# Stick-breaking attention layer: start of the kernel reordered, parked splits moved in the queues, some VectorE work moved to GpSimd

## The chip, the cores and the metric

The kernel runs on one core of a Trainium2 chip. The metric is device time in microseconds (us) of one launch. The engines of the core are TensorE (PE in the profile, PEld for its weight loads), VectorE (DVE), ScalarE (ACT) and GpSimd (POOL). SyncE (SP) only issues transfers (DMAs). Every engine works its own instructions in the order of the program and waits for the others by semaphores.

## What is computed

One layer of an encoder (DEPTH is 1, so only mixer 0 is used) on 2048 tokens of 1024 features, all float32:

```python
def stick_breaking_mixer(h, w_qkv, w_o):
    qkv = (h @ w_qkv).reshape(b, s, 3, N_HEADS, HEAD_DIM)
    q, k, v = qkv[:, :, 0], qkv[:, :, 1], qkv[:, :, 2]
    ...
        z = jnp.einsum('bthd,bshd->bhts', q[:, q0:end], k[:, :end]).astype(jnp.float32) * scale
        ...
        sp = jnp.where(mask, jax.nn.softplus(z), 0.0)
        rest = lax.cumsum(sp, axis=3, reverse=True)
        log_a = jnp.where(mask, z - rest, -jnp.inf)
        a = jnp.exp(log_a).astype(v.dtype)
        outs.append(jnp.einsum('bhts,bshd->bthd', a, v[:, :end]))
    ...
    return o @ w_o
...
    mod_all = jnp.einsum('bd,lde->lbe', jax.nn.silu(c), ada_w) + ada_b[:, None]
    ...
        sh_m, sc_m, gt_m, sh_f, sc_f, gt_f = jnp.split(mod_all[i][:, None, :], 6, axis=-1)
        h = modulate(rms_norm(x, norm_g[i, 0]), sh_m, sc_m)
        y = stick_breaking_mixer(h, sb_w_qkv[r], sb_w_o[r])
        x = x + gt_m * rms_norm(y, norm_g[i, 1])
        h = modulate(rms_norm(x, norm_g[i, 2]), sh_f, sc_f)
        y = swiglu_ffn(h, ffn_w_in[i], ffn_w_out[i])
        x = x + gt_f * rms_norm(y, norm_g[i, 3])
```

There are 16 heads of 64 features (8 pairs of heads), and the FFN is 2816 wide.

## The kernel before, in words

**Splits.** Products keep float32 accuracy by splitting each operand into a high part (a cast to fp32r, mostly on ACT) and a low part (operand minus high part, mostly on DVE); `mm3` then makes three matmuls for each product (its three are lines 254 to 256). Tokens stand in four blocks of 512 (b = 0 to 3), heads in eight pairs (p = 0 to 7).

**The start (from line 988).** The first transfers bring c, the biases and gains of the modulation, x of block 0, c as one row, and rows of the modulation's weights mixed with the first weights of q, k and v. PE runs `warm` matmuls, whose result nobody reads, spreads c over all partitions (`c_spread`, line 1016), and runs more of them. `x_square` (ACT, line 245), a power on GpSimd (249) and `x_scale` (DVE, 433) normalize x. `row_sum` (881) and `column` (873) make the shift and scale of one block of 128 features after another; `turn_x`, `full`, `high`, `low` make the modulated input h, and `products(p, m)` adds feature block m into the q, k and v of token block 0, for head pairs 0 and 1 at once (`EARLY`). `weights_high` and `weights_low` split the weights, in two halves of features each.

**The parked pair.** The q, k and v of (p=1, b=0) are made at the start but used much later. `project` splits them by functions put on the list `waiting` and stores them to DRAM (`k_park`, `q_park`, `v_s`); `unpark` brings them back. The v of head pair 1 stands in a tile with the tag `vn`, of which there is **one buffer** (`BUFS["vn"]` is 1): `take_values(b, half, acc)` copies the high parts on ACT (line 716) and makes the low parts on DVE (718) for pair 0 and pair 1, and after the second half it issues the store of pair 1's tile (722). The next block's `take_values` writes the same buffer, and so waits for that store.

**Order.** PE, ACT, DVE and GpSimd run what is written, in that order. `project(at)` yields one slice after each feature block; t = 1 is k, t = 0 is q, t = 2 and 3 are the halves of v. `at` = 2 is (p=0, b=1). Within it `X_AT` and `NORM_AT` hang the norm of blocks 2 and 3 on slices (squares, scales, loads, and `first_norm`, which turns and modulates one feature block). SP's transfers all go through one hardware queue; their order is the scheduler's.

**After attention.** `out_projection(b)` multiplies by w_o; beside it `o_load`, `o_add`, `o_prep` add and split the two partial attention outputs of the next block, `y_square`, `y_gate`, `y_norm`, `x1_add`, `x1_square`, `x1_scale`, `h2_turn` make the residual and the FFN's input. The FFN follows, with `end_square`, `end_mean`, `end_norm`, `end_store` at its end.

Of the kernel before, what the change touches and what calls it, by code (L numbers as in the profile page):

```python
# [11 lines left out]
AF = mybir.ActivationFunctionType  # L12
ALU = mybir.AluOpType
# [133 lines left out]

NORM_IN_KEYS = {1: {0: 4, 1: 5, 2: 6, 3: 7}, 2: {0: 5, 1: 6, 3: 7}, 3: {0: 5, 1: 6, 3: 7}}

H_FETCH_AT = [0, 2, 4, 6]  # L150
# [3 lines left out]
def f32(ap):  # L154
    return ap.bitcast(F32)
# [22 lines left out]
def hybrid_trunk_kernel(  # L178
# [20 lines left out]
    nc = tc.nc  # L199
# [11 lines left out]
    ones = const.tile([P, P], F32, name="ones")  # L211
# [59 lines left out]
    raws = {}  # L271
# [271 lines left out]
    def project(at):  # L543
# [17 lines left out]
        def product(t):  # L561
# [3 lines left out]
            for k in range(KC):  # L565
                if t == 1 and p == 0:
                    first_norm(b, NORM_IN_KEYS[b].get(k, KC))
                    if k >= 4 and waiting:
                        waiting.pop(0)()
                for what, *which in X_AT.get((at, t, k), []):  # L570
# [53 lines left out]
        def split(acc, tag):  # L624
            place = "wraw" if parked else "qkn"
            hl = att.tile([P, 2, BT], F32R, name=f"{tag}n{p}_{b}", tag=place, bufs=BUFS[place])
            nc.scalar.copy(hl[:, 0], acc)
            nc.vector.tensor_tensor(hl[:, 1], acc, f32(hl[:, 0]), op=ALU.subtract)
            return hl
# [4 lines left out]
        if parked:  # L634
            for out_of in held:
                nc.sync.dma_start(*out_of)
            for t, to in ((1, k_park), (0, q_park)):
                waiting.append(
                    lambda t=t, to=to: nc.sync.dma_start(to, f32(split(first_acc[p, t], "qk"[t])))
                )  # L640
            for half in range(2):
                waiting.append(lambda half=half: take_values(0, half, first_acc["v", half]))
            return
# [283 lines left out]
    def weights_low(half, *which):  # L927
        ks = K_HALVES[half]
        for of in which:
            if of == "v":  # L930
                hl = value_split[half]
                nc.vector.tensor_tensor(hl[:, 1], raws.pop(("v", 0, half)), f32(hl[:, 0]), op=ALU.subtract)
                continue
            p, t = of
            hi, lo = weights[p, t]
            raw = raws[p, t] if half == 0 else raws.pop((p, t))
            nc.vector.tensor_tensor(lo[:, ks], raw[:, ks], f32(hi[:, ks]), op=ALU.subtract)

# [49 lines left out]
    c_line = att.tile([P, D], F32, name="c_line", tag="qkn", bufs=BUFS["qkn"])  # L988
    nc.vector.memset(c_line, 0.0)
    nc.sync.dma_start(c_act, c)  # L990
    nc.sync.dma_start(b_cols, ada_b_cols)
    nc.sync.dma_start(gc, g_cols)
    x_load(0, 0)
    x_load(0, 1)
    nc.sync.dma_start(c_line[0:1], c_row)
    x_load(0, 2)
    x_load(0, 3)
    pairs = [[(0, 1), (0, 0)], [(1, 1), (1, 0), "v"]]
    row_load(0)
    weights_load(0, *pairs[0])  # L1000
    row_load(1)
    weights_load(0, *pairs[1])
# [12 lines left out]
    for half in range(2):  # L1015
        nc.tensor.matmul(c_spread[half], ones, c_line[:, c_halves[half]], start=True, stop=True)
    warm(11)
    x_square(0, 0)
    x_square(0, 1)
    x_scale(0, 0)  # L1020
    c_rows = att.tile([P, D], F32, name="c_rows", tag="qkn", bufs=BUFS["qkn"])
    for half in range(2):
        nc.scalar.activation(c_rows[:, c_halves[half]], c_spread[half], AF.Sigmoid)
    for half in range(2):
        nc.vector.tensor_tensor(
            c_rows[:, c_halves[half]], c_spread[half], c_rows[:, c_halves[half]], op=ALU.mult
        )
    x_scale(0, 1)
    x_square(0, 2)
    row_sum(0, 0)  # L1030
    x_square(0, 3)
    x_scale(0, 2)
    row_sum(0, 1)
    x_scale(0, 3)
    row_done(0)
# [3 lines left out]
    }  # L1039
    weights_high(0, *pairs[0])  # L1040
    turn_x(0)
    turn_x(1)
    full(0)
    weights_low(0, *pairs[0])
    high(0)
    low(0)
    acol = zps.tile([P, BT], F32, name="acol", tag="z")
    column(1, 0)
    products(0, 0)
    column(1, 1)  # L1050
# [62 lines left out]
    low(5)  # L1113
    x_load(2, 0, 1)
    store(2)
# [14 lines left out]
    high(7)  # L1130
    x_load(2, 2, 3)
    products(0, 5)
# [89 lines left out]
    def y_gate(i):  # L1222
        t = y_gated[0, i, 0]
        nc.vector.tensor_tensor(t, t, gate[0], op=ALU.mult)

# [46 lines left out]
    def o_add(b, k):  # L1272
        parts = o_parts.pop((b, k))
        o = att.tile([P, BT], F32, name=f"of{b}_{k}", tag="tmp", bufs=BUFS["tmp"])
        eng = nc.vector if b else nc.gpsimd
        eng.tensor_tensor(o, parts[:, 0], parts[:, 1], op=ALU.add)
        o_sum[b, k] = o
# [548 lines left out]
    def end_norm(s, i, j):  # L1826
        rstd = att.tile([P, 1], F32, name=f"e{s}_{i}_{j}_rstd", tag="rms_rstd", bufs=4)
        ms = att.tile([P, 1], F32, name=f"e{s}_{i}_{j}_sum", tag="rms_ms2", bufs=4)
        nc.vector.tensor_scalar(
            ms, end_ssq.pop((s, i, j)).pop(), end_ms.pop((s, i, j)), None, op0=ALU.add  # L1830
        )
        nc.gpsimd.tensor_tensor(rstd, ms, mhalf, op=ALU.pow)
        end_rstd[s, i, j] = rstd
# [140 lines left out]
```

## Time and profile before

| what | value |
|---|---|
| median of 3 runs | 2821.14 us (2820.8 to 2825.9) |
| the profiled execution's own time | 2822.93 us |
| its span | 2821.1 us |
| mean granted TensorE clock | 0.999 |
| DVE, ACT, POOL busy | 72%, 57%, 45% of the span |
| HBM | 360.48 MB read, 128.45 MB written, 173 GB/s over the span |

Each row of a profile's groups or timeline has the line of the kernel, the engine, the operation and what it writes and reads (out<-in, with buffer numbers left out), then busy time and idle time before it with the instruction or transfer that ended the idle time. Table rows by stretch give the busy microseconds of each engine, the granted clock, the share of the 16 DMA engines that was busy, and GB/s.

### The profile page before, as it was taken

The numbers are of one execution on the slowest core, as the hardware profiler recorded it, in microseconds if no ns is written. First come the engines' busy times: TensorE is split into PE (matmuls) and PEld (weight loads), VectorE is DVE, ScalarE is ACT, GpSimd is POOL, SyncE is SP. The second block draws the span as 40 slices with busy tenths as digits, with TensorE's granted clock in tenths as the row PEclk, the third lists the DMA queues.
The fourth block names the chain that finished last, engine by engine and source line by source line (L and its number), as shares of the span: only waits on it lengthen the run. The fifth ranks groups of instructions, "written<-read, shape, count | busy, mean of one in ns | idle before, by whom it ended". The sixth has DMA issues, their size and how long they took to land.

```text
span 2821.1 us, 42833 instructions
## 1 busy us (share of the span) xinstructions
PE 2787.4 (99%) x14297; PEld 2351.6 (83%) x14297; DVE 2024.4 (72%) x2841; ACT 1620.9 (57%) x3262; POOL 1276.2 (45%) x2031
## 2 busy tenths in 40 slices
PE   9999999999999999999999999999999999999998
PEld 7888888888888888888787888888888888888887
DVE  7788898888898888889767766555786665133467
ACT  5687777777787878788645533334433334322343
POOL 1475666666676656667310122222222222544454
PEclk9999999999999999999999999999999999999999
DMA  9866567786678745364489545335363335645565
GB/s 376 309 218 195 152 220 230 226 267 222 197 260 271 229 144 189 122 202 157 140 286 316 169 150 160 106 112 168 119 191 111 91 112 164 197 143 151 179 226 186
DMA packets 252096, 540.53 MB, mean 192 GB/s; under 512 B 23393, under 2 KB 117601, under 8 KB 234978
## 3 DMA queue, kind: packets, MB, share of 16 engines
q1 hardware_dynamic: 251874, 537.78, 59.2%
q8 instruction: 113, 1.85, 0.3%
q14 instruction: 109, 0.89, 0.1%
HBM read 360.48 MB, written 128.45 MB: 173 GB/s over the span
## 4 chain that ended last, share of the span: by engine, by line
PE 81%; DMA 6%; DVE 6%; issue 3%; POOL 2%; ACT 2%; SPq 1%; DVEq 0%; POOLq 0%; ACTq 0%
PE s L254 9%; PE s L256 9%; PE s L255 9%; PE o L837 8%; PE z L758 8%; PE t L809 8%; PE pj L254 5%; PE pj L256 5%; PE pj L255 5%; PE o L255 4%; PE o L256 4%; PE o L254 4%; DMA xc<-in_xt 1%; PE y L256 1%; PE y L254 1%
## 5 line engine op out<-in xcount | busy, mean ns | idle before, releaser
L799 POOL TENSOR_TENSOR a<-a,w 128x512 f32<-128x512 f32 (+3 forms) x640 | 620.0, 969 | 221.5 <-DVE w L792 121.4
L792 DVE TENSOR_TENSOR_SCAN w<-z,c,begin 128x512 f32<-128x512 f32 x384 | 488.7, 1278 | 76.0 <-ACT z L777 62.1
L254 PE MATMUL s<-r,l 128*128 128x512 f32 x1232 | 481.4, 391 | 1.6 <-ACT p L1647 1.4
L256 PE MATMUL s<-r,l 128*128 128x512 f32 x1232 | 479.6, 389 | 0.0
L255 PE MATMUL s<-r,l 128*128 128x512 f32 x1232 | 479.4, 389 | 0.0
L775 ACT ACTIVATE a<-z 128x512 f32<-128x512 f32 (+3 forms) x640 | 347.4, 543 | 165.0 <-PE z L758 141.5
L837 PE MATMUL o<-aT,v 128*128 128x512 f32 (+3 forms) x1280 | 384.6, 382 | 0.0
L825 DVE TENSOR_TENSOR aT<-t,aT 128x512 fp32r<-128x512 f32 (+3 forms) x640 | 358.9, 596 | 19.8 <-ACT aT L819 18.8
L758 PE MATMUL z<-kt,qt 128*128 128x512 f32 (+3 forms) x1280 | 363.1, 365 | 0.6 <-DVE n_ms L247 0.6
L819 ACT CAST aT<-t 128x512 fp32r<-128x512 f32 (+3 forms) x640 | 312.7, 533 | 77.7 <-PE t L809 62.1
L777 ACT ACTIVATE z<-z 128x512 f32<-128x512 f32 (+3 forms) x640 | 345.0, 539 | 0.0
L1711 POOL TENSOR_TENSOR one<-p,p 128x512 f32<-128x512 f32 x44 | 70.5, 1603 | 574.4 <-issue 303.7
L809 PE MATMUL t<-begin,a 128*128 128x128 f32 x2176 | 295.7, 273 | 9.9 <-DVE aT L825 8.4
L809 PEld LDWEIGHTS t<-begin,a 128*128 128x128 f32 x2176 | 252.8, 140 | 52.7 <-DVE aT L825 12.5
L254 PEld LDWEIGHTS s<-r,l 128*128 128x128 f32 x1232 | 231.3, 188 | 51.4 <-ACT p L1647 2.2
L256 PEld LDWEIGHTS s<-r,l 128*128 128x128 f32 x1232 | 231.3, 188 | 48.4 <-DVE l L1564 0.4
L255 PEld LDWEIGHTS s<-r,l 128*128 128x128 f32 x1232 | 231.3, 188 | 48.2 <-issue 0.5
L758 PEld LDWEIGHTS z<-kt,qt 128*128 128x128 f32 x1280 | 230.2, 188 | 38.3 <-DVE n_ms L247 1.0
L787 DVE TENSOR_TENSOR_SCAN w<-z,begin 128x128 f32<-128x128 f32 (+3 forms) x256 | 208.3, 817 | 73.5 <-ACT z L777 57.7
L1564 DVE TENSOR_TENSOR l<-ls,l 128x512 fp32r<-128x512 f32 x172 | 129.5, 753 | 155.0 <-ACT l L1563 154.7
L837 PEld LDWEIGHTS o<-aT,v 128*128 128x128 f32 x1280 | 214.2, 190 | 23.8 <-issue 0.7
L254 PE MATMUL pj<-ht,w 128*128 128x512 f32 x576 | 230.0, 399 | 0.2 <-DVE ht L481 0.2
(195 smaller groups left out, 5373.1 us busy)
## 6 DMA issues: line engine op xcount, KB each, us to landing
ht<-h_s SPq DMA_DIRECT2D x108, 1024.0 KB, 7.7
wi<-in_win SPq DMA_DIRECT2D x86, 512.0 KB, 4.3
qt<-qn SPq DMA_DIRECT2D x124, 256.0 KB, 4.4
ol_qt<-act_s SPq DMA_DIRECT2D x56, 512.0 KB, 3.8
act_s<-S SPq DMA_DIRECT2D x66, 256.0 KB, 5.0
br<-in_wout SPq DMA_DIRECT2D x66, 256.0 KB, 3.6
h_s<-ht SPq DMA_DIRECT2D x16, 1024.0 KB, 10.0
o_s<-os SPq DMA_DIRECT2D x128, 128.0 KB, 3.2
```

The source lines that it names most:

```text
L254: nc.tensor.matmul(acc, lhs[0], rhs[0], start=first, stop=False, **kw)
L255: nc.tensor.matmul(acc, lhs[0], rhs[1], start=False, stop=False, **kw)
L256: nc.tensor.matmul(acc, lhs[1], rhs[0], start=False, stop=last, **kw)
L758: nc.tensor.matmul(z[:, :n], q[:, e, part, r * P : (r + 1) * P], k[:, e, :n], start=part == 0, stop=part == 1,)
L775: nc.scalar.activation(a[:, :n], z[:, :n], AF.Sigmoid, scale=QK_SCALE)
L777: nc.scalar.activation(z[:, :n], z[:, :n], AF.Sigmoid, scale=-QK_SCALE)
L792: nc.vector.tensor_tensor_scan(rest[:, rev], left[:, rev], begin[:, :BT][:, rev], initial=carries[r], op0=ALU.mult, op1=ALU.bypass,)
L799: nc.gpsimd.tensor_tensor(a[:, :n], a[:, :n], rest[:, 1 : n + 1], op=ALU.mult)
L809: nc.tensor.transpose(pt[:, rb * P : (rb + 1) * P], weighed[i, rb][:, j * P : (j + 1) * P], ident)
L819: nc.scalar.copy(hl[:, 0, t0:], pt[:, t0:])
L825: nc.vector.tensor_tensor(hl[:, 1, t0:], pt[:, t0:], f32(hl[:, 0, t0:]), op=ALU.subtract)
L837: nc.tensor.matmul(acc[:, t0:], lhs, hl[:, part, t0:], start=sc == qb and j == 0 and part == 0, stop=sc == 0 and j == 3 and part == 1,)
```

## The change

The start: the order of the first transfers, of the squares, of the weight splits and of one `column` is changed, c is spread with one row of ones instead of 128, two of the `x_scale` go to ACT, two `warm` matmuls go, and the second halves of the weights' low parts are made on GpSimd. The parked splits: their slices are given by `WAITING_AT` (at, t, k), values first, and their tiles have the tag `aT` instead of `wraw`. After attention: `y_gate` and, for block 1, `o_add` go to GpSimd, and the sum in `end_norm` too.

```diff
+WAITING_AT = [(2, 0, 1), (2, 0, 4), (2, 2, 0), (2, 2, 3)]
...
                 if t == 1 and p == 0:
                     first_norm(b, NORM_IN_KEYS[b].get(k, KC))
-                    if k >= 4 and waiting:
-                        waiting.pop(0)()
+                if (at, t, k) in WAITING_AT:
+                    waiting[WAITING_AT.index((at, t, k))]()
...
         def split(acc, tag):
-            place = "wraw" if parked else "qkn"
+            place = "aT" if parked else "qkn"
...
-            for t, to in ((1, k_park), (0, q_park)):
-                waiting.append(
-                    lambda t=t, to=to: nc.sync.dma_start(to, f32(split(first_acc[p, t], "qk"[t])))
-                )
-            for half in range(2):
-                waiting.append(lambda half=half: take_values(0, half, first_acc["v", half]))
+            park = lambda t, to: nc.sync.dma_start(to, f32(split(first_acc[p, t], "qk"[t])))
+            waiting.extend([
+                lambda: take_values(0, 0, first_acc["v", 0]), lambda: park(1, k_park),
+                lambda: park(0, q_park), lambda: take_values(0, 1, first_acc["v", 1]),
+            ])
             return
...
-                nc.vector.tensor_tensor(hl[:, 1], raws.pop(("v", 0, half)), f32(hl[:, 0]), op=ALU.subtract)
+                eng = nc.gpsimd if half else nc.vector
+                eng.tensor_tensor(hl[:, 1], raws.pop(("v", 0, half)), f32(hl[:, 0]), op=ALU.subtract)
...
-            nc.vector.tensor_tensor(lo[:, ks], raw[:, ks], f32(hi[:, ks]), op=ALU.subtract)
+            eng = nc.gpsimd if half else nc.vector
+            eng.tensor_tensor(lo[:, ks], raw[:, ks], f32(hi[:, ks]), op=ALU.subtract)
...
-    nc.vector.memset(c_line, 0.0)
     nc.sync.dma_start(c_act, c)
-    nc.sync.dma_start(b_cols, ada_b_cols)
-    nc.sync.dma_start(gc, g_cols)
-    x_load(0, 0)
-    x_load(0, 1)
     nc.sync.dma_start(c_line[0:1], c_row)
-    x_load(0, 2)
-    x_load(0, 3)
+    for i in range(4):
+        x_load(0, i)
     pairs = [[(0, 1), (0, 0)], [(1, 1), (1, 0), "v"]]
     row_load(0)
     weights_load(0, *pairs[0])
+    nc.sync.dma_start(b_cols, ada_b_cols)
+    nc.sync.dma_start(gc, g_cols)
...
-        nc.tensor.matmul(c_spread[half], ones, c_line[:, c_halves[half]], start=True, stop=True)
-    warm(11)
-    x_square(0, 0)
-    x_square(0, 1)
-    x_scale(0, 0)
+        nc.tensor.matmul(c_spread[half], ones[0:1], c_line[0:1, c_halves[half]], start=True, stop=True)
+    warm(9)
...
+    for i in range(4):
+        x_square(0, i)
+    x_scale(0, 0)
     x_scale(0, 1)
-    x_square(0, 2)
+    for i in range(2, 4):
+        nc.scalar.activation(x_norm[0, i], x_tiles.pop((0, i)), AF.Identity, scale=x_rstd.pop((0, i)))
     row_sum(0, 0)
-    x_square(0, 3)
-    x_scale(0, 2)
     row_sum(0, 1)
-    x_scale(0, 3)
     row_done(0)
...
-    weights_high(0, *pairs[0])
+    weights_high(0, pairs[0][0])
     turn_x(0)
     turn_x(1)
     full(0)
-    weights_low(0, *pairs[0])
+    weights_low(0, pairs[0][0])
     high(0)
+    weights_high(0, pairs[0][1])
     low(0)
+    weights_low(0, pairs[0][1])
     acol = zps.tile([P, BT], F32, name="acol", tag="z")
+    products(0, 0)
     column(1, 0)
-    products(0, 0)
     column(1, 1)
...
-    x_load(2, 0, 1)
...
-    x_load(2, 2, 3)
+    x_load(2)
...
     def y_gate(i):
         t = y_gated[0, i, 0]
-        nc.vector.tensor_tensor(t, t, gate[0], op=ALU.mult)
+        nc.gpsimd.tensor_tensor(t, t, gate[0], op=ALU.mult)
...
-        eng = nc.vector if b else nc.gpsimd
+        eng = nc.vector if b > 1 else nc.gpsimd
...
-        nc.vector.tensor_scalar(
-            ms, end_ssq.pop((s, i, j)).pop(), end_ms.pop((s, i, j)), None, op0=ALU.add
-        )
+        nc.gpsimd.tensor_tensor(ms, end_ssq.pop((s, i, j)).pop(), end_ms.pop((s, i, j)), op=ALU.add)
         nc.gpsimd.tensor_tensor(rstd, ms, mhalf, op=ALU.pow)
```

Three places in the order of the instructions. In the rows, `kn_1`, `qn_1` and `v_1` are of token block 1, `kn_0`, `qn_0` and `v_0` (the two buffers of `take_values`, pair 0 and pair 1) are the parked ones of block 0; x_0 to x_3 are four token tiles.

SP's queue from the last stores of h of block 1 on, before (`h_s_107` is h of block 2, `x_0` to `x_2` here are x of block 3):

```order
L523 DMA h_s_106<-ht_1_3_773 128x2048
L639 DMA k_park<-kn_0_785 128x1024
L639 DMA q_park<-qn_0_799 128x1024
L722 DMA v_s_0_85<-v_0_813 128x1024
L653 DMA kt_1_846<-kn_1_843 64x512 x4
L410 DMA x_0_853<-in_x 128x1024
L410 DMA x_1_855<-in_x 128x1024
L410 DMA x_2_857<-in_x 128x1024 x2
L662 DMA qt_1_898<-qn_1_895 64x1024 x4
L523 DMA h_s_107<-ht_2_0_879 128x2048
```

The same stretch of SP's queue in the changed kernel:

```order
L525 DMA h_s_106<-ht_1_3_770 128x2048
L654 DMA kt_1_824<-kn_1_821 64x512 x4
L412 DMA x_0_831<-in_x 128x1024
L412 DMA x_1_833<-in_x 128x1024
L412 DMA x_2_835<-in_x 128x1024 x2
L639 DMA k_park<-kn_0_857 128x1024
L663 DMA qt_1_886<-qn_1_883 64x1024 x4
L639 DMA q_park<-qn_0_892 128x1024
L525 DMA h_s_107<-ht_2_0_867 128x2048
L723 DMA v_s_0_85<-v_0_842 128x1024
```

The store of the parked v (`v_s_0`) moved from the third transfer after h of block 1 to the last of these, behind keys, x of block 3, queries and one store of h of block 2.

ACT around the parked values in the changed kernel (lines 717 and 482 are 716 and 480 of before):

```order
L717 CAST v_0_841<-pj_0_2_370 128x4x64
L717 CAST v_0_842<-pj_0_2_370 128x4x64
L717 CAST v_1_959<-pj_1_2_891 128x4x64
L717 CAST v_1_960<-pj_1_2_891 128x4x64
L482 ACTIVATE hf_2_982<-xT_2_983,mod,g_eff 128x512
L482 ACTIVATE hf_3_1003<-xT_3_1004,mod,g_eff 128x512
L776 ACTIVATE a_0_1020<-z_0_978 128x128
```

and the same stretch before:

```order
L716 CAST v_0_812<-pj_0_2_373 128x4x64
L716 CAST v_0_813<-pj_0_2_373 128x4x64
L245 ACTIVATE xj_789,n_2_3_ssq<-x_3_639 128x1024
L627 CAST kn_1_843<-pj_1_1_758 128x512
L480 ACTIVATE hf_0_880<-xT_0_881,mod,g_eff 128x512
L627 CAST qn_1_895<-pj_1_0_851 128x512
L480 ACTIVATE hf_1_916<-xT_1_917,mod,g_eff 128x512
L716 CAST v_1_962<-pj_1_2_903 128x4x64
L716 CAST v_1_963<-pj_1_2_903 128x4x64
L480 ACTIVATE hf_2_985<-xT_2_986,mod,g_eff 128x512
```

Five instructions that stood between the parked values' second half and block 1's values now stand ahead of it; nothing of ACT is left between the two.

PE at the start, before (`acol` is `column`, the pj rows are `products`):

```order
L459 MATMUL xT_1_313<-begin,xn_3_289 128x128
L873 MATMUL acol<-c_act,ar_213 128x1 x8
L254 MATMUL pj_0_0_301<-ht_0_0_322,w_1_304 128x512
L255 MATMUL pj_0_0_301<-ht_0_0_322,w_1_304 128x512
L256 MATMUL pj_0_0_301<-ht_0_0_322,w_1_304 128x512
```

and now:

```order
L461 MATMUL xT_1_308<-begin,xn_3_282 128x128
L256 MATMUL pj_0_0_298<-ht_0_0_316,w_1_301 128x512
L257 MATMUL pj_0_0_298<-ht_0_0_316,w_1_301 128x512
L258 MATMUL pj_0_0_298<-ht_0_0_316,w_1_301 128x512
L256 MATMUL pj_0_1_299<-ht_0_0_316,w_0_318 128x512
```

The first `column` no longer stands between the transposes of x and the first products.

## The prediction

> **What bounds the kernel now.** First the page's busy times and the table by stretch (columns: PE, PEld, DVE, ACT, POOL busy, granted clock, DMA share, GB/s).
>
> ```profile
> PE 2787.4 (99%) x14297; PEld 2351.6 (83%) x14297; DVE 2024.4 (72%) x2841; ACT 1620.9 (57%) x3262; POOL 1276.2 (45%) x2031
> ...
> 40.00:60.00 20.00, 19.24 (x117) 16.83 (x116) 15.73 (x37) 11.53 (x19) 2.30 (x4) 1.00 1.02 419
> 60.00:70.00 10.00, 9.85 (x44) 7.62 (x43) 8.45 (x18) 8.11 (x16) 1.65 (x3) 1.00 1.03 340
> 70.00:80.00 10.00, 7.38 (x51) 6.37 (x51) 6.38 (x12) 2.90 (x6) 1.25 (x2) 1.00 1.00 418
> 80.00:90.00 10.00, 8.36 (x71) 8.16 (x71) 3.25 (x7) 2.88 (x7) 0.04 (x1) 1.00 0.94 324
> 90.00:100.00 10.00, 9.26 (x52) 7.13 (x50) 8.48 (x16) 9.61 (x21) 4.55 (x10) 1.00 1.03 330
> 100.00:110.00 10.00, 9.66 (x51) 8.04 (x52) 7.66 (x15) 5.64 (x15) 5.85 (x11) 1.00 1.02 416
> ```
>
> PE is the bound: 2787.4 of 2821.1 us. An edit on another engine counts only where PE waits for it, and a PE stall is not made up later. PE has little to lose: 33.7 us idle in all. The change touches three places where it is idle: the start, the stretch from 70 to 115 us, and the output projection near 1390 us. In the second the DMA engines are full (share 0.94 to 1.03 until 110 us) while PE, DVE and ACT all have room. So there I look for a transfer that somebody waits for: the chain of waits (start, us, what), ACT's timeline, then PE's.
>
> ```profile
> 72.87 12.74 DMA v_s<-v
> ...
> 96.37 11.76 DMA xc<-in_xt
> ...
> 81.71 0.37 ACT L716 CAST v<-pj 128x256 fp32r<-128x256 f32 x1 [3.53 <-PE pj L256]
> 85.71 0.37 ACT L716 CAST v<-pj 128x256 fp32r<-128x256 f32 x1 [3.63 <-DMA v_s<-v]
> 85.98 0.78 ACT L480 ACTIVATE hf<-xT,mod,g_eff 128x512 f32<-128x512 f32 x1
> ...
> 86.82 0.66 PE L459 MATMUL xT<-begin,x 128*128 128x128 f32 x4 [1.64 <-ACT hf L480]
> ```
>
> This is the one-buffer tag `vn` at work. The store of the parked v is issued at 72.87 and takes 12.74 us, because megabytes stand ahead of it. ACT finishes the first half of block 1's values at about 82.1, then waits for the store (85.61) before it may overwrite the tile; everything behind on ACT waits too, and PE's next transposes start at 86.82, **1.21 us after the store has landed**. PE lost 1.64 us to it.
>
> **The change part by part: the parked store.** The order rows ahead show the store moved in SP's queue: still behind h of block 1, k_park and q_park, but now also behind `kt_1`, x of block 3, `qt_1` and one store of h. The view of DMA issues gives the sizes (KB for one issue, median us to landing):
>
> ```profile
> h_s<-ht SPq DMA_DIRECT2D x7, 1024.0 KB, 11.2
> x<-in_x SPq DMA_DIRECT2D x4, 512.0 KB, 8.3
> v_s<-v SPq DMA_DIRECT2D x2, 512.0 KB, 12.2
> qt<-qn SPq DMA_DIRECT2D x4, 256.0 KB, 10.1
> ...
> kt<-kn SPq DMA_DIRECT2D x4, 128.0 KB, 10.8
> ```
>
> New ahead of it: kt 4 x 128, x 4 x 512, qt 4 x 256, one h_s of 1024: 4608 KB = 4.5 MB (of 1024 KB). The price of a megabyte comes from two landings in the chain. v_s lands at 72.87 + 12.74 = 85.61, the first xc at 96.37 + 11.76 = 108.13. Between them in the queue of before stand kt_1 (0.5), x (2), qt_1 (1), three stores of h (3), v_s of block 1 (0.5) and the first xc (0.5): 7.5 MB in 22.52 us, **3.0 us each**. The store lands 4.5 x 3.0 = 13.5 us later, at 99.1. At the fastest row above (419 GB/s, 2.50 us for a megabyte) it is 11.3 us, at the slower 330 GB/s of 90 to 100 us (3.18) 14.3 us. I take 13.5, since that is the mean over the same mix of transfers.
>
> Can ACT arrive later than that? No: the parked values' second half now hangs on slice (2,2,3) and block 1's first half follows about four slices later, near 81 us. So **ACT will wait some 17 us instead of 3.63**. Queued behind it: `hf_2` and all further h of block 2, the first sigmoids of attention, the second half of the values. PE runs on to the same transposes (near 85 us) and stops there. It resumes at 99.1 + 1.2 = 100.3 instead of 86.82: **+13.5 us**.
>
> What the change wins ahead of that place is swallowed by it, since the landing, not PE's arrival, ends the wait. This goes for the squares of block 2, which no longer alternate with parked splits on ACT (the waits of PE by cause):
>
> ```profile
> PE xT L459 <- DVE x L433: 2.6, 4, 1.1
> PE z L758 <- DVE n_ms L247: 0.6, 1, 0.6
> PE t L809 <- DVE aT L825: 0.7, 1, 0.7
> PE pj L255 <- DVE n_ms L247: 0.2, 1, 0.2
> PE pj L254 <- DVE ht L481: 0.2, 1, 0.2
> ```
>
> Of the 2.6 us at 71 to 74 us perhaps half goes, and nothing of it is left at 100 us. What is late next is only what comes after: the scores at 98.60 waited 0.6 us as the queries of block 1 had landed late, and the 0.7 us at 112.20 ended a chain that began with xc landing. Both transfers then land early against PE. I take **-1.3 us**, between 0 and -1.7 (the four rows behind the first, all of them after 98 us).
>
> After some 15 us of rest PE may come back slow. At the start it does:
>
> ```profile
> 1.31 4.21 PE L984 MATMUL idle<-begin,ones 128*128 128x384 f32 x6 [1.31 <-POOL begin L208]
> ...
> 7.37 3.56 PE L1016 MATMUL cs<-c_line,ones 128*128 128x512 f32 x4 [1.85 <-DMA c_line<-in_c_row]
> ...
> 10.77 7.26 PE L984 MATMUL idle<-begin,ones 128*128 128x384 f32 x22
> ```
>
> The same matmul took 0.70 us first and 0.33 us from 10.77 on: from 7.37 to there 3.4 us at half rate, 1.7 us lost. No rest later in this trace is long enough to show whether a warm PE cools, so the bounds are 0 and 3.4 (twice that ramp). I take **+1.7**. The Trainium skill, TensorE: Matmul & The Clock Gate, section What's actually happening, says that it does, after an idle window of about 3.4 us; by it the term stays and its lower bound goes, which no run here shows yet.
>
> **The start.** c arrives before the bulk, so `c_spread` starts when the first warm matmuls end, 5.52 instead of 7.37, and ends near 9.1. But ACT now does the sigmoids of c first and then all four squares, and DVE does all means ahead of the first scale.
>
> ```profile
> 12.50 1.05 ACT L245 ACTIVATE xn<-x 128x1024 f32<-128x1024 f32 x1
> ...
> 15.25 1.22 DVE L881 SCALAR_TENSOR_TENSOR ar<-ar,c_rows 128x1024 f32<-128x1024 f32 x1
> ...
> 17.26 0.16 DVE L888 SCALAR_TENSOR_TENSOR g_eff<-mod,gc 128x1 f32<-128x1 f32 x1
> ...
> 18.73 1.84 PE L873 MATMUL acol<-c_act,ar 128*128 128x1 f32 x16
> ...
> 20.44 0.48 PE L254 MATMUL pj<-ht,w 128*128 128x512 f32 x1
> ...
> 40.82 0.55 POOL L249 TENSOR_TENSOR n_rstd<-n_ms,mhalf 128x1 f32<-128x1 f32 x1 [25.44 <-DVE mod L887]
> ```
>
> 9.1, a sigmoid half as wide as a square (0.6, an estimate), and four squares of 1.05 make 13.9; DVE's means, two scales, two row sums of 1.22 and the rest take some 4.5 us behind them: g_eff near 18.4 against 17.42. The first product then starts near 20, about as now, but without the 1.84 us of `column` that filled the wait ahead of it and now follows. PE is behind by some 1.4 us (from -1 if the clock rises sooner, to 1.8). The five low parts that go to GpSimd (four 128x512, one twice as wide: some 8 us by the 1.40 us row below) run while it stands idle, up to 40.82 us; DVE has that much less. All of this ends in the same wait at 85 us: **0**, or 1 either way through the queue.
>
> **The output projection.** `of` and the gate of yh leave DVE (DVE's timeline, PE's, then two groups by line: PE's transposes of h2 from 1340 to 1420 us, and the same `of` where GpSimd makes it already, for block 0 from 1250 to 1300 us).
>
> ```profile
> 1383.65 0.68 DVE L1276 TENSOR_TENSOR of<-op 128x512 f32<-128x512 f32 x1
> ...
> 1386.18 0.69 DVE L825 TENSOR_TENSOR aT<-t,aT 128x512 fp32r<-128x512 f32 x1
> ...
> 1386.92 0.66 PE L809 MATMUL t<-begin,a 128*128 128x128 f32 x4 [1.65 <-DVE aT L825]
> 1400.40 0.50 PE L254 MATMUL y<-wo,ohl 128*128 128x512 f32 x1 [1.47 <-DVE yt L1217]
> ...
> L1253 PE MATMUL h2T<-begin,x1n 128*128 128x128 f32 x12 | 2.0, 277 | 0.6 <-DVE x1n L1246 0.6
> ...
> L1276 POOL TENSOR_TENSOR of<-op 128x512 f32<-128x512 f32 x8 | 11.2, 1400 | 0.0
> ```
>
> At 1386.92 PE waits for aT, ahead of which DVE runs without a break from 1383.04; one `of` less (a start to start of 0.60) brings it 0.6 us earlier. The same at 1400.40 through yt, and once more for the 0.6 us of h2T: **-1.8 us**. All three waits gone would be -3.7. GpSimd's 1.40 us for one `of` hides, as the split that needs it is asked for three slices later, and GpSimd's other work there is a power now and then. In `end_norm` an addition of 128x1 changes engines ahead of a power on GpSimd; 0.2 us either way at the end.
>
> Sum: 13.5 - 1.3 + 1.7 + 0 - 1.8 = **+12.1 us**. The profiled execution took 2822.93 us; it would take 2835.0. The median shown is 1.8 us lower, so I predict **2833.2 us**. The bounds together: 11.3 - 1.7 + 0 - 1 - 3.7 = +4.9, and 14.3 + 3.4 + 1 + 1 = +19.7; as not all fall on one side at once, 2827 to 2839.
>
> **Rivals.**
> 1. *Faster: the store does not decide.* If the transfers do not land in the order of issue, a small store can pass the 4.5 MB. It must land before ACT is there, near 81 us, for PE to run through. Then the waits 2.6 (half of it), 1.64, 1.3 and 1.8 go: -6 us, 2815. For it: nothing orders them but the queue. Against it: v_s took 12.74 us in a full queue, as long as the bytes ahead need. The Trainium skill, DMA: Bandwidth & Descriptors, section Two DMAs through the same engine are not ordered, says that nothing orders transfers across the 16 engines; but each has its ring, and the trace's latency shows a full ring, so it gives this rival a chance and no more.
> 2. *No difference to be measured:* the store lands only some 5 to 8 us later, because the queue runs faster or emptier when the transfers come from loads that are ready early (340 GB/s in 60 to 70 us leaves room); with the wins -1.3 and -1.8 the sum is +2 to +5: 2823 to 2826.
> 3. *The same wait, and GpSimd blocks DVE.* The eight `of` and four gates on GpSimd (12 x about 1.2 us) hold DVE up rather than relieve it; the -1.8 becomes +3: 2838. The row for it is below: a 0.74 us operation took 1.30 beside a GpSimd one.
>
> ```profile
> 109.45 1.30 DVE L469 SCALAR_TENSOR_TENSOR xc<-xc,g_eff,xv 128x512 f32<-128x512 f32 x1 [0.41 <-DMA xc<-in_xt]
> 110.67 0.74 DVE L487 SCALAR_TENSOR_TENSOR ht<-xc,mod,ht 128x512 fp32r<-128x512 f32 x1
> ```
>
> The Trainium skill, SBUF — State Buffer, section Who interferes with whom, says that a DVE operation with two SBUF inputs and a GpSimd one exclude each other for a whole instruction. By it this rival would be the rule; most DVE work there reads PSUM or has room, so I keep it small.
>
> **How the numbers follow.** My forecast 0.62, rival 3 0.10, rival 2 0.18, rival 1 0.10. The range takes in the forecast, rival 3 and most of rival 2: 2823 to 2839. A measurement of this kernel can tell about 0.2%, 5.6 us, from no change. Slower by more (above 2826.8): forecast, rival 3 and a little of rival 2, 0.74. Within: rival 2 and half of rival 1, 0.20. Faster (below 2815.5): 0.06.
>
> **What would show it.** Right: v_s issued near 88 and landing near 99 us; ACT's line 717 with one wait of 15 to 18 us; PE idle over 12 us near 85 to 100; slow matmuls just after. Right at the projection: PE's waits at 1387 and 1400 shorter by 0.6. Wrong: v_s landing before 90, or ACT's wait under 8 us.

## The result and the profile after

| what | before | after |
|---|---|---|
| median | 2822.9 us of 6 (2820.6 to 2826.5) | 2843.4 us of 6 (2839.6 to 2845.0) |
| ratio | 1 | 1.007, 95% interval 1.0057 to 1.0083 |
| span of the profiled execution | 2821.1 us | 2840.6 us |
| mean granted clock | 0.999 | 0.994 |
| v_s lands, PE resumes | 85.61, 86.82 us | 103.14, 104.34 us |

The change is slower, as forecast, but by 20.5 us instead of some 12; the time is 4.4 us above the range. The page's busy times of the changed kernel, then its table by stretch (columns as before: PE, PEld, DVE, ACT, POOL, granted clock, DMA share, GB/s):

```profile
PE 2795.1 (98%) x14293; PEld 2358.9 (83%) x14293; DVE 2017.4 (71%) x2805; ACT 1622.8 (57%) x3264; POOL 1310.5 (46%) x2064
```

```profile
20.00:30.00 10.00, 10.00 (x43) 9.45 (x42) 5.49 (x12) 2.62 (x4) 0.00 (x0) 0.50 1.03 403
30.00:40.00 10.00, 10.00 (x54) 9.04 (x53) 8.37 (x12) 5.42 (x9) 6.03 (x4) 0.82 0.88 346
...
80.00:90.00 10.00, 9.68 (x82) 9.48 (x81) 3.68 (x7) 2.77 (x6) 0.00 (x0) 1.00 1.00 347
90.00:100.00 10.00, 0.00 (x0) 0.00 (x0) 0.00 (x0) 0.00 (x0) 0.00 (x0) 0.75 1.02 361
100.00:110.00 10.00, 5.66 (x31) 5.66 (x32) 3.38 (x8) 3.10 (x7) 0.45 (x2) 0.57 0.89 347
```

Two things are new. From 90 to 100 us no engine does anything while the DMA engines are full: the forecast stall. And from 20 to 30 us PE is "busy" all the time at **half the clock**, which the trace of before does not have between 10.6 us and its last matmul: a busy PE that gets half as much done. The mean clock of 0.994 hides it. The stall in the chain of waits (start, us, what), on ACT and on PE:

```profile
93.57 9.57 DMA v_s<-v
```

```profile
86.22 0.37 ACT L717 CAST v<-pj 128x256 fp32r<-128x256 f32 x1 [2.99 <-PE pj L258]
103.24 0.37 ACT L717 CAST v<-pj 128x256 fp32r<-128x256 f32 x1 [16.65 <-DMA v_s<-v]
```

```profile
85.18 0.28 PE L258 MATMUL pj<-wv,ht 128*128 128x256 f32 x1
...
104.34 1.12 PE L461 MATMUL xT<-begin,x 128*128 128x128 f32 x4 [14.66 <-ACT hf L482]
...
105.69 0.41 PE L258 MATMUL pj<-wv,ht 128*128 128x256 f32 x1
```

PE goes on 1.20 us after the landing (1.21 before), and its matmul of 256 columns takes 0.41 us after the rest against 0.28 before it. The start, in PE's timeline:

```profile
15.37 0.77 PE L461 MATMUL xT<-begin,xn 128*128 128x128 f32 x5 [0.78 <-ACT xn L1030]
18.36 0.49 PE L256 MATMUL pj<-ht,w 128*128 128x512 f32 x1 [2.22 <-ACT ht L971]
...
20.74 6.82 PE L874 MATMUL acol<-c_act,ar 128*128 128x1 f32 x32
```

The first product comes at 18.36 instead of 20.44 us, earlier than forecast. But ahead of it PE stands still for 2.22 us where `column` had been, and the two columns now run back to back: 32 matmuls of one column each at 0.213 us, where 16 took 1.84 us (0.115 each) before. At the output projection the waits of PE are

```profile
1406.99 0.65 PE L810 MATMUL t<-begin,a 128*128 128x128 f32 x4 [2.38 <-DVE aT L826]
1419.87 0.50 PE L256 MATMUL y<-wo,ohl 128*128 128x512 f32 x1 [0.87 <-DVE yt L1216]
1426.20 0.50 PE L258 MATMUL y<-wo,ohl 128*128 128x512 f32 x1 [0.80 <-DVE ohl L1283]
```

in place of 1.65, 1.47 and 0.59 (h2T): 4.05 against 3.71 us.

### The profile page after: what moved, and what is told of

The parts are those of the page before. It is cut to its first block, busy times and chain, and to the rows that moved or that the text cites. A ratio compares the mean times of both kernels' runs of the same rounds, so it can differ in the third digit from the quotient of the medians.

```text
span 2840.6 us, 42832 instructions
## 1 busy us (share of the span) xinstructions
PE 2795.1 (98%) x14293; PEld 2358.9 (83%) x14293; DVE 2017.4 (71%) x2805; ACT 1622.8 (57%) x3264; POOL 1310.5 (46%) x2064
## 4 chain that ended last, share of the span: by engine, by line
PE 83%; DVE 6%; DMA 4%; issue 3%; ACT 2%; POOL 2%; SPq 0%; DVEq 0%; POOLq 0%; ACTq 0%
PE s L256 9%; PE s L257 9%; PE s L258 9%; PE z L759 8%; PE o L838 8%; PE t L810 8%; PE pj L256 5%; PE pj L257 5%; PE pj L258 5%; PE o L258 4%; PE o L256 4%; PE o L257 4%; PE y L258 1%; PE y L256 1%; PE y L257 1%
## 5 line engine op out<-in xcount | busy, mean ns | idle before, releaser
L810 PEld LDWEIGHTS t<-begin,a 128*128 128x128 f32 x2176 | 252.7, 140 | 53.5 <-DVE aT L826 13.5
```

The costliest lines, as they stand in the source:

```text
L810: nc.tensor.transpose(pt[:, rb * P : (rb + 1) * P], weighed[i, rb][:, j * P : (j + 1) * P], ident)
```

## Experiments

**One part at a time.** The change has three parts: the start (S), the parking (P), and the work after attention on GpSimd (O). Four kernels hold P alone, S alone, O alone, and S with O. The edits are those of the diff, made singly; S with O is the changed kernel with the list `waiting` in its old order and with

```diff
-                if (at, t, k) in WAITING_AT:
-                    waiting[WAITING_AT.index((at, t, k))]()
+                    if k >= 4 and waiting:
+                        waiting.pop(0)()
...
-            place = "aT" if parked else "qkn"
+            place = "wraw" if parked else "qkn"
```

P alone:

> The kernel before with only the parked splits changed (new slices, values first, tag aT). Theory A: v_s lands 13.4 us later, near 99 us, PE resumes near 100.2 instead of 86.82 with a wait of 13 to 16 us, and then runs at half clock for some 4 us: 2823 + 13.4 + 2.1 - 0.3 = about 2838. Rival (most of the 20 us come from the new start, which shifts the transfers into a worse time; the parking alone costs the 5 to 8 us that a queue with some air would give): 2828 to 2831. Rival (no cooling of the clock without the dip at the start): 2836.

S with O:

> The changed kernel with the parked splits as they were (their old slices, their old order k, q, v, v, their old tag); the new start and the new work on GpSimd stay. Theory A (the moved store costs 13.4 us of transfers and 2.1 us of half clock after the rest; the new start costs some 4 us that pass through the queue; the projection and the end are near nothing): 2843.4 - 15.5 = about 2828, that is 4 to 6 us over before; the stall of PE at the first h_2 of block 2 is 1 to 3 us, near 91 us, and v_s lands near 89.5 instead of 85.61. Rival S0 (the start is worth nothing by itself, the late arrival only came together with the new parking): 2822 to 2824. Rival S+ (the start saves time that the new parking hid): under 2820.

O alone:

> The kernel before with only the gates of yh, the sums of block 1 in the output projection and the sum at the end on GpSimd. The prediction's step: PE's waits at 1387 and 1400 us get 0.6 shorter each, the 0.6 for h2T goes: -1.8, about 2821. The rival from the trace of the changed kernel: the waits in the projection add up to 0.8 us more than before (2.4 instead of 1.65 at the transposes of a, 0.8 new at the split of o), and the tail is 1.4 us shorter: between -1 and +0.5, 2822 to 2823.5. The prediction's third rival (GpSimd holds DVE up for whole instructions): +3, 2826.

S alone:

> The kernel before with only the new start (transfers, squares, splits, columns, GpSimd's halves). From the two runs with the new start without the new parking and with both: half clock for 10 to 14 us from about 20 us on, the first store of h of block 1 lands near 77.5 to 78 us, v_s near 89.5, PE resumes near 90.7: +4 us, 2826 to 2827. Rival (the 5 us of the first run came from the projection's part): 2822 to 2823.

| kernel | median | ratio to before, 95% interval | PE resumes |
|---|---|---|---|
| P alone | 2838.7 us | 1.0058 (1.0045 to 1.0071) | 101.09 us |
| S alone | 2828.5 us | 1.0025 (1.0015 to 1.0035) | 90.83 us |
| O alone | 2824.9 us | 1.0008 (0.9999 to 1.0017) | 88.04 us, no wait |
| S with O | 2829.0 us | 1.0024 (1.0015 to 1.0033) | 90.74 us |

P alone costs 16.6 us over its own runs of before (2822.1), as theory A had it. In its trace the view of the tile v_s, "who waited for it", and PE's timeline say why:

```profile
  ACT v L717: 19.0, 1
```

```profile
101.09 1.12 PE L461 MATMUL xT<-begin,x 128*128 128x128 f32 x4 [16.98 <-ACT hf L482]
```

PE resumes 14.3 us later than before, and the clock's records are at half until 105.0, 3.9 us more, half of it lost: 16.2 of the 16.75 us by which the transposes at 1379 us are late. S alone costs 6.0 us: there the first store of h of block 1 lands at 77.07 us (before 73.31) and v_s at 89.63 (85.61), and PE resumes 4.0 us later; the rest gathers behind that, 1.5 us in small waits up to 1450 us and 1.4 us in a window of half clock at 1517.56 us. O alone is +2.7 by its median, with an interval that reaches zero; in its trace PE is already 1.2 us late at the first product of the output projection (1303.20 instead of 1302.01 us), ahead of all that the edit touches and behind half clock from 73.15 to 79.98 us, which the trace of before does not have in the same instructions.

The three sum to some 25 us and the change costs 20.5. Where PE resumes little of that is lost (14.27 and 4.01 us alone, 17.52 together). A window of half clock near 1515 us stands in S alone and in O alone, and only once in the changed kernel. What is left of the difference lies within the three intervals.

**The wait itself.** Two edits of the changed kernel. One gives the parked values another buffer, so that the store may be as late as it likes; the other moves the store up in the queue.

```diff
-            for pair, tag in enumerate(("v", "vn")):
+            for pair, tag in enumerate(("v", "vn" if b else "aT")):
```

> The changed kernel, but the parked values of pair 1 of block 0 stand in a tile of the tag aT (four buffers) instead of vn, so that block 1's values need not wait for the store of the parked ones; the store keeps its late place in the queue. Theory A (the store's landing, through the one buffer of vn, is what stops ACT and with it PE): the wait of 16.65 us at line 717 and PE's 14.66 us go, the half clock behind them goes, and the time falls by 15 to 17 us to 2826 to 2828. Rival T (the transfers themselves are late for everybody: the h of block 2, keys and x of block 3 in the fuller queue would stop PE next): PE waits at least 5 us for another transfer between 85 and 115 us, 2832 or more.

```diff
-WAITING_AT = [(2, 0, 1), (2, 0, 4), (2, 2, 0), (2, 2, 3)]
+WAITING_AT = [(2, 0, 1), (2, 0, 2), (2, 0, 4), (2, 2, 0)]
...
-                lambda: take_values(0, 0, first_acc["v", 0]), lambda: park(1, k_park),
-                lambda: park(0, q_park), lambda: take_values(0, 1, first_acc["v", 1]),
+                lambda: take_values(0, 0, first_acc["v", 0]),
+                lambda: take_values(0, 1, first_acc["v", 1]),
+                lambda: park(1, k_park), lambda: park(0, q_park),
```

> The changed kernel with the parked splits in the order v, v, k, q (slots 2,0,1, 2,0,2, 2,0,4 and 2,2,0), so that the store of the parked values takes the place in the queue that k_park has now: behind keys and x of block 3 only. Theory A (the price is that of the bytes ahead of the store): v_s lands where k_park landed, near 94.8 instead of 103.14 us, PE resumes near 96 instead of 104.34, time 8 us less, 2834 to 2836. Rival (the new tag aT or the order on ACT and DVE causes the wait): v_s lands earlier, but the time stays above 2840.

With the other buffer: 2827.5 us, **15.9 us less** than the changed kernel, although the store lands at 104.64, later than ever. With the store moved up: 2834.1 us, 9.3 less. The tile view of the first has nobody left who waits (nothing stands between these two of its lines); PE's timeline of the second shows what remains:

```profile
who waited for it (us, times):
busy tenths in 40 slices 0000000000000000000000000000000000000000
```

```profile
95.92 1.11 PE L461 MATMUL xT<-begin,x 128*128 128x128 f32 x4 [6.23 <-ACT hf L482]
```

Its v_s lands at 94.71, 8.4 us earlier, and PE resumes 1.2 us after it as in the changed kernel. So it is neither the tag aT nor the order on ACT and DVE but the place in the queue together with the one buffer. PE stopped for no other transfer in place of that one (with the other buffer its longest wait from 85 to 120 us is 1.84 us, for aT at 115.9): theory T falls.

**The clock at the start.** In the changed kernel the first column was put ahead of the products again:

```diff
-    products(0, 0)
     column(1, 0)
+    products(0, 0)
```

> The changed kernel with the first column of the modulation's second block ahead of the first products again: the 16 small matmuls fill PE's wait of 2.22 us at 16 us. Theory A (that gap lets the clock fall to half from 19.9 to 33.5 us, and the 4.1 us by which the first store of h of block 1 lands late come from there): the granted clock stays full from 20 to 33 us, the first store of h of block 1 lands near 73.5 to 74.5 instead of 77.40, v_s near 99 to 100 instead of 103.14, and the time is 3 to 4 us less, about 2839.5 to 2840.5. Rival (the start is late by the order of the first transfers and by the splits on GpSimd, the clock only happens beside it): the same landings as in the changed kernel within 1 us, 2843.

2840.0 us, and the landings came as expected (73.85 and 100.65 us), but the clock did not: it was at half from 18.3 to 28.6 us though PE's wait was down to 0.53 us (PE's timeline):

```profile
15.26 1.84 PE L874 MATMUL acol<-c_act,ar 128*128 128x1 f32 x16
17.64 0.49 PE L256 MATMUL pj<-ht,w 128*128 128x512 f32 x1 [0.53 <-ACT ht L971]
18.36 0.79 PE L257 MATMUL pj<-ht,w 128*128 128x512 f32 x1 [0.23 <-DVE ht L975]
```

The landing came back without the clock because three things add up: the first product is 0.72 us earlier, sixteen one-column matmuls (1.7 us) stand in the wait again, and there are 3.41 us less of half clock (1.7 us). PE is 4.10 us earlier at its third group of transposes (29.34 instead of 33.44 us), and 3.55 us of that reach the store.

The rows had PE busy for 79% of the 3.41 us ahead of the fall. Without the one-column matmuls it is 30%, and so counted the falls of six runs had at most 0.45 in the 3.41 us ahead of them. From this came theory C, tried on S alone with useless matmuls, `fill(n)`, written to a part of the `acol` tile that nobody reads: once 7 in the gap with the columns still in a row, once 3 with the column ahead.

```diff
+    fill(7)
...
     products(0, 0)
     column(1, 0)
     column(1, 1)
```

> The new start alone with 7 useless matmuls of 384 columns, as long as PE's wait of 2.22 us ahead of the first products, written ahead of them; the two columns (32 matmuls of one column each) still stand in a row behind the products. Theory C, from the clock's records of six runs: the clock is judged by windows of 3.41 us, a window in which PE's work without the one-column matmuls is below about 0.4 is followed by half clock. By it the two columns in a row (3.4 us at full clock) are such a window themselves: half clock still comes, 2 to 6 us later than in the new start alone, and the time is 0 to 2 us less than there, 2824 to 2827. Rival I (only time without any matmul counts): the clock stays full from 6 us on, v_s lands near 85.5 and the time is about 2821 to 2822.

```diff
+    fill(3)
...
+    column(1, 0)
     products(0, 0)
-    column(1, 0)
     column(1, 1)
```

> The new start alone with the first column ahead of the products again, apart from the second, and 3 useless matmuls of 384 columns ahead of it, so that no window of 3.41 us has less than about half of other work. Theory C and rival I: the clock stays full from about 6 us on; the first product starts near 18 us instead of 20.44 in the kernel before, the first store of h of block 1 lands near 71.5 to 73.5, v_s at 84 to 86; 2820 to 2822, 5 us less than the new start alone. Rival (the start is late by its transfers or by GpSimd's splits): within 1.5 us of the new start alone, 2825 to 2827.

The stretches of S alone (first fence) and of S with the gap filled (second):

```profile
15.70:19.11 3.41, 0.97 (x4) 0.53 (x4) 2.40 (x7) 2.56 (x5) 0.00 (x0) 1.00 1.04 414
19.11:22.52 3.41, 3.41 (x15) 3.03 (x13) 3.40 (x5) 1.35 (x2) 0.00 (x0) 0.50 1.02 408
```

```profile
19.14:22.55 3.41, 3.41 (x20) 2.73 (x19) 3.40 (x5) 1.31 (x2) 0.00 (x0) 1.00 1.03 410
22.55:25.96 3.41, 3.41 (x31) 3.32 (x31) 1.04 (x5) 0.32 (x1) 0.00 (x0) 1.00 1.05 392
25.96:29.37 3.41, 3.41 (x14) 3.02 (x13) 3.32 (x8) 3.24 (x6) 0.17 (x1) 0.50 1.03 407
```

With the gap filled PE is busy in every row, and the clock falls all the same, right behind the window in which the columns ran (PE's timeline of that kernel):

```profile
15.61 4.68 PE L992 MATMUL acol<-begin,ones 128*128 128x384 f32 x14
...
21.52 3.63 PE L873 MATMUL acol<-c_act,ar 128*128 128x1 f32 x32
```

That speaks for theory C against rival I. At the start it fell for one window instead of four, and once more at 77.16 us (the trace is of the fastest of ten executions, 2824.2 us). The filling was longer than meant (7 came to 14 matmuls and 4.68 us, so that the products started 1.8 us later than in S alone), and the time, 2827.8 us, is within C's expectation but for 0.8 us, and no test of it. With the column ahead and apart, the lowest window at the start had 0.48, the clock stayed full through the start to 42.3 us, the first store of h of block 1 landed at 73.14 us (S alone 77.07, before 73.31), v_s at 85.01, and nobody waited for it: 2824.9 us (ratio to before 1.0011, 1.0002 to 1.0020), **3.6 us less than S alone**. I had expected 2820 to 2822. The rest is not settled; its trace shows PE waiting for the norm of block 1, which the kernel before did not:

```profile
40.74 0.66 PE L459 MATMUL xT<-begin,xn 128*128 128x128 f32 x4 [1.27 <-ACT hf L959]
42.76 0.79 PE L255 MATMUL pj<-ht,w 128*128 128x512 f32 x1 [0.88 <-DVE n_ms L247]
```

and two windows of half clock, at 42.30 and at 76.44 us. Behind the second window PE reaches at 88.14 us, without a wait, the transposes that the kernel before reached at 86.82.

**The projection.** Only the sums, then only the gates, on GpSimd, in the kernel before:

```diff
-        eng = nc.vector if b else nc.gpsimd
+        eng = nc.vector if b > 1 else nc.gpsimd
```

> The kernel before with only the sums of block 1 in the output projection on GpSimd; the gates of yh stay on DVE. In the run with both, DVE's residual add took 1.75 instead of 0.75 us and its split 1.06 instead of 0.69 us while GpSimd worked on the gate (1.73 us), and PE's wait at the transposes of a grew from 1.65 to 2.39 us. Theory G (the gate holds DVE up): without it that wait is 1.0 to 1.1 us as the prediction said, and the time is 0.5 to 1.5 us less than before, 2821 to 2822. Rival (the sums hold DVE up): the wait is still above 2 us.

```diff
-        nc.vector.tensor_tensor(t, t, gate[0], op=ALU.mult)
+        nc.gpsimd.tensor_tensor(t, t, gate[0], op=ALU.mult)
```

> The kernel before with only the gates of yh on GpSimd. Theory G (GpSimd's gate, an operation with two SBUF inputs, holds up DVE's operations with SBUF inputs beside it): DVE's residual add takes 1.5 us or more beside it instead of 0.75, PE's wait at the transposes of a is 2.2 to 2.4 us instead of 1.65, time 0.5 to 1.5 us over before, 2823 to 2824. Rival (it relieves DVE as the prediction said): the wait is 1.65 or less, 2821 to 2822.5.

| PE waits for (us) | before | sums alone | gates alone | O alone | after |
|---|---|---|---|---|---|
| aT, transposes of a | 1.65 | 1.37 | 1.66 | 2.39 | 2.38 |
| yt | 1.47 | 0.87 | 1.47 | 0.87 | 0.87 |
| ohl | | 0.37 | 0.43 | 0.82 | 0.80 |
| x1n, first h2T | 0.59 | 0.83 | | | |
| sum | 3.71 | 3.44 | 3.56 | 4.08 | 4.05 |

The times, 2821.1 us (0.9998, 0.9989 to 1.0007) and 2821.8 us (0.9998, 0.9989 to 1.0007), cannot be told from before; the waits can. Theory G is half right. With the gates alone DVE's residual add at 1404.13 us did take 1.77 us beside a gate (1403.98 to 1405.36). But the wait for aT stayed at 1.66 us: there the gate ran from 1381.29 to 1382.66 us, when DVE was idle but for 0.23 us. For the wait of 2.38 us it takes both edits. DVE's timeline of the changed kernel, then GpSimd's:

```profile
1402.33 0.69 DVE L826 TENSOR_TENSOR aT<-t,aT 128x512 fp32r<-128x512 f32 x1 [3.05 <-ACT aT L820]
1402.94 1.06 DVE L1283 TENSOR_TENSOR ohl<-of,ohl 128x512 fp32r<-128x512 f32 x1
1403.92 1.76 DVE L1231 SCALAR_TENSOR_TENSOR xr<-yh,y_rstd,xr 128x512 f32<-128x512 f32 x1
```

```profile
1399.66 3.79 POOL L1275 TENSOR_TENSOR of<-op 128x512 f32<-128x512 f32 x3
1403.40 1.72 POOL L1223 TENSOR_TENSOR yh<-yh,gate 128x512 f32<-128x512 f32 x1
```

DVE's `ohl` ends at 1404.00, 0.55 us behind the third sum (1403.45), and its residual add at 1405.68, 0.56 behind the gate (1405.12). Neither reads what GpSimd was making just then: `ohl` takes the second sum, whose high part ACT cast from 1402.19 us on, and the add takes the result of the first gate, made from 1393.75 to 1395.05 us. So DVE did not wait for data. It was held until GpSimd's operation had ended. All nine traces with one of these edits show it: between 1365 and 1440 us each of the 30 operations `of`, `ohl` and `xr` of DVE that began beside a sum or a gate ended 0.55 us behind it, and took 1.06 to 1.78 us instead of 0.67 to 0.75. Both inputs of these stand in SBUF, the memory of the tiles. `aT`, one of whose inputs is PE's result in PSUM, the memory that PE writes, kept its 0.69 us beside the third sum. The three sums of 1.29 us ahead of the gate in GpSimd's queue are what put the gate beside the add.

**Both good edits together** in the kernel before, the other buffer and the sums:

> The kernel before with two edits: the parked values of pair 1 in a tile of the tag aT, so that the wait of 3.63 us on ACT and 1.64 us on PE near 86 us goes, and the sums of block 1 on GpSimd (0.6 us). If nothing takes the place of the wait: 2 us less than before, 2820 to 2821. Rival (PE comes to xc, q and k of block 1 that much earlier and waits there): 2821.5 to 2822.5.

2822.1 us, ratio 0.9998 (0.9989 to 1.0007): no difference. The wait at 86 us is gone from its trace, and PE reaches the transposes at 1377.79 instead of 1379.14, but 1.35 us is less than these medians can tell. The time is the rival's; its reason, that PE waits there instead, is not in the trace, where PE is 1.3 to 1.9 us early from 85 us on. No version here is measurably faster than the kernel before.

## Why the prediction was wrong

Of its own list, ACT's one wait (16.65 us), PE's idle time (14.66 us) and the slow matmuls behind it came true, v_s was issued 5.6 and landed 4.0 us later than it said, and of the two waits at the projection one grew.

- **The parked store, +13.5: right.** Counted from the first store of h of block 1 in the same queue, v_s landed 25.74 us later (77.40 to 103.14) against 12.30 before (73.31 to 85.61): +13.44. That this is within 0.1 us of the forecast is luck, as with the column back the same transfers took 26.80 us; the size is not. Alone, PE resumed 14.3 us later. Taking the wait away by a buffer gave 15.9 us back, with the clock's share in it.
- **The cold clock after the rest, +1.7: right.** Half clock until 108.61, 4.3 us after PE resumed: 2.1 us, inside 0 to 3.4. The Trainium skill, TensorE: Matmul & The Clock Gate, section What's actually happening, says that an idle window of about 3.4 us cools PE; the trace agrees, with 14.66 us of idle PE and half clock from 94.96 us on.
- **The start, 0: the step that failed.** It read "All of this ends in the same wait at 85 us: 0, or 1 either way through the queue". The new start alone costs 6.0 us, 4.0 of them through this wait. I reckoned with PE's arrival but not with its clock: the first column stood in a gap and was moved into a row with the second. The gap of 2.22 us and the row of one-column matmuls brought 13.65 us of half clock, a term that the sum did not have. PE's third group of transposes, before and then after:

```profile
26.95 0.60 PE L459 MATMUL xT<-begin,xn 128*128 128x128 f32 x4
```

```profile
33.44 0.64 PE L461 MATMUL xT<-begin,xn 128*128 128x128 f32 x4
```

These 6.5 us are 2.1 us won at the first product, 1.7 lost by the sixteen matmuls that had stood in the gap, and 6.9 lost by the half clock. Some 2.4 us were made up ahead of the stores; the first two stores of h landed 4.1 us late (77.40 and 79.84 us) in the full queue, and the wait ends with the queue. With the column back PE was 2.4 us late at the same place and the first store 0.54; in S with the gap filled it was 2.9 and 2.0. So 0.8 to 2.4 us of a delay are absorbed, and the rest passes through to the end of the wait. The other terms missed by less: 2.1 us at the projection, 1.0 at the later waits, and some 1.5 us in a window of half clock at 1532 us that no term had.

- **Later waits recovered, -1.3: too much.** After the stall the trace still has 0.625, 0.197, 0.229 and 0.449 us of waits where before had 0.572, 0.211, 0.224 and 0.749: 0.3 recovered. They were not the transfers'; with the other buffer PE still waits 0.56 us for n_ms at the scores.
- **The projection, -1.8: wrong sign in sum.** The wait for yt fell by 0.60 as worked out, and h2T's went, but that for aT grew by 0.73 and one for ohl came: +0.34. The sum priced the relief and put the hold-up at nothing: in the changed kernel four operations of DVE (one `ohl`, three adds) took 3.4 us longer in all beside sums and gates. My cover, "asked for three slices later", is about data, and in the rows shown the data were there.
- **Rivals.** Rival 1 (small stores pass) and 2 (5 to 8 us) fell. Rival 3 had the right place and the right mechanism: GpSimd held DVE up for whole operations. But PE lost 0.3 us by it in sum and not 3.
- **The end, 0.2 either way: right.** From the start of DVE's last gate to that of its last multiplication it is 1.14 us (before 1.27). In the sum of the upper bounds, 14.3 + 3.4 + 1 + 1, the second 1 belongs to no term that the prediction works out.

Two things stay open. The new start with the gap filled and the column ahead still costs 2.4 us (by the interval of the ratio 0.6 to 5.6); its trace has 6.8 us of half clock behind the start, and its other parts (the order of the transfers, the loads of x of block 2 at once, the splits on GpSimd) were not tried apart. And 3.41 us of half clock, worth up to 1.7 us, stand at 1532 us in the changed kernel and as late in seven of the twelve other kernels, O alone, S alone and the sums alone among them, but not in the kernel before. They follow PE waits of 2.23 to 2.73 us (before 1.79). With P alone the wait there was 2.50 us, with the gap filled 3.05 us, and the clock stayed full, so the fall is tied neither to one edit nor to the length of the wait.

## What to carry to other kernels

A store that frees a single buffer is a dependency: count the bytes that a reordering puts ahead of it, at the queue's own price, and ask who writes that buffer next. Read the granted clock by stretches of a few microseconds beside PE's busy time, since a PE that is busy at half clock looks full; what fills a gap must be wide matmuls (384 columns did it here, one column did not). Work moved to an idle engine can hold up the engine that it leaves: look at what each operation will run beside, and not only at who waits for its result.

## What the runs showed of the hardware

- The clock falls and rises in steps of 3.41 us: the 13.65, 10.24, 17.07 and 3.41 us of half clock are 4, 3, 5 and 1 of them. Counted over the fourteen traces, from full clock and up to the last matmul, it fell behind all 23 steps in which matmuls wider than one column filled at most 0.41 of PE's time (0.37 in the changed kernel's start, 0.29 in S alone, 0.28 with the gap filled) and behind none above 0.55. Between 0.43 and 0.55 it fell four times (0.45, 0.50 and twice 0.55) and more often did not, so the limit is not sharp. The Trainium skill, TensorE: Matmul & The Clock Gate, section What's actually happening, speaks of a free-running window of that length and agrees with these steps; that a whole idle window is needed does not agree, since a gap of 2.2 us did it, and in one kernel no gap at all.
- One-column matmuls do not hold the clock: 32 of them kept PE busy for 3.6 us from 21.52 us on (S with the gap filled), and it fell behind them.
- Whether a gap lets the clock fall depends on how it lies in the steps. At the same h2T, a wait of 2.48 us (O alone) took 2.15 us out of one step and brought a fall; one of 3.05 us (gap filled) was split by the end of a step into 1.39 and 1.66 us and brought none. So executions of the same instructions differ: before, O alone, the sums alone and the gates alone are the same program up to 1300 us, and from 12 us on to there the clock stayed full in the first, fell once in the third (75.43 us) and for two steps in the two others (73.15 and 73.38 us).
- A DVE operation with both inputs in SBUF that begins beside a sum or a gate on GpSimd ends 0.55 us behind it (30 of 30 in nine traces), and one with an input in PSUM is not held. The other way round, the gate of 1403.40 us took 1.72 us instead of 1.29 beside `ohl`, which ran until 1404.00.
- The price of the full queue held: 13.44 us for 4.5 MB is 2.99 us for a megabyte, as the 3.0 worked out from before; with the column back it was 14.50 us, 3.2 for a megabyte.
